# Splitting each weights' unit in one instruction per part instead of two, with a ring of two whole units

## The chip, the cores and the metric

One core of one Trainium2 chip runs the whole program. The metric is the device time of one execution in microseconds (us); of several executions the median counts. The engines are named as in the profile: PE is TensorE (PEld its weight loads), DVE is VectorE, ACT is ScalarE, POOL is GpSimd, and SP issues the DMA transfers.

## The reference

The input is 256 tokens of width 1024 in float32, batch 1. Two transformer-like stacks follow each other. The first has two layers: a mixer of a state-space branch and a neighbourhood attention, then an mLSTM mixer, each followed by an MLP. The second has one layer of three mixers, a cross attention and a gated MLP. What matters here is that nearly all of the work is a product of 256 tokens with a large float32 matrix:

```python
proj = h @ w_in                                          # mixers
u = jnp.square(jax.nn.relu(h @ mlp_w1[layer])) @ mlp_w2[layer]   # MLP of the first stack
a, b = jnp.split(h @ w_gu, 2, axis=-1)                   # gated MLP of the second stack
return (jax.nn.silu(a) * b) @ w_d
```

## The kernel before

**Units.** All weight matrices are cut on the host into 214 units of 128 partitions x 2048 float32 (1 MB each), in the order in which the program uses them. A unit is 256 columns of a matrix with 1024 rows, or 256 rows of one with 1024 columns. `unit(u, n)` brings one in: SP issues the DMA into a buffer `raw` (three of them, shared with the modulation weights `in_ada`), ACT writes a rounded copy `wh` (the high part, type fp32r), and DVE writes `wl = raw - wh` (the low part). A product of float32 accuracy is then made of three matmuls: high by high, high by low, low by high. The activations are split in the same way (`xh`, `xl`, or `mhh`, `mhl`, `ghh`, `ghl`, `yh`, `yl`).

**The ring.** `wh` and `wl` come from two pools that are used in rotation over the whole program. Before, a unit's part is two tiles of 1024 columns, and each pool has four tiles (`W_BUFS = 4`). A tile can be written again when the last matmul that reads it is done. 14 units (`fwh`, `fwl`: the fillers between the stages and some first units) have buffers of their own.

**The matmuls of a unit.** `proj_feat` and `proj_tok` make 48 matmuls of 256 columns: an outer loop over two halves of the output, an inner one over the eight blocks k of 128 rows, of which blocks 0 to 3 lie in the first tile and 4 to 7 in the second. So the first tile is read for the last time after 36 of the 48 matmuls, the second after all 48. `down` makes 24 matmuls of 512 columns, and there too the first tile is free after 18 of 24. `out_units` runs the last two units of a mixer's output matrix together: 12 matmuls of the one, 12 of the other, and then both again.

**The order.** The code is traced from top to bottom, and a scheduler then orders the instructions of each engine; each engine runs its own in order. Side work (state-space heads, attention heads, modulation vectors from `in_ada`, tables) is given out in steps between the units by `tick`. `held` keeps the first splits of a stage behind the last instructions of the norm before it, for all units but those marked `free` or with buffers of their own.

**Stages by time in the profile.** Start to 70 us, mixer0 70 to 272, norm and mlp0 272 to 490, mixer1 490 to 722, mlp1 722 to 925, mixer2 925 to 1250, cross attention to 1318, and the gated MLP to the end. In the MLPs an up unit (48 matmuls into `mm`) and a down unit (24 matmuls into `ax`) alternate; in the gated MLP there are two up units for one down unit.

Of the kernel before, what the change touches and what calls it, by code (L numbers as in the profile page):

```python
# [12 lines left out]
F32R = mybir.dt.float32r  # L13
I32 = mybir.dt.int32
AF = mybir.ActivationFunctionType
ALU = mybir.AluOpType
# [3 lines left out]
P = 128  # L20
# [2 lines left out]
NEG = -1.0e30  # L23
NOSYNC = mybir.DependencyInfo(mybir.DependencyClass.NoSync, mybir.DependencyReason.DATA)
RAW_BUFS = 3
W_BUFS = 4
NB_BUFS = 4

M0_ORDER = "aaaxxxaaaxbzaaazaaazz"
# [239 lines left out]
class Stack:  # L269
    def __init__(self, ctx, tc, aps):  # L270
# [3 lines left out]
        self.raw_p = pool("raw", RAW_BUFS)  # L274
        self.wh_p = pool("wh", W_BUFS)
        self.wl_p = pool("wl", W_BUFS)
        self.xT_p = pool("xT", 1)
# [153 lines left out]
    def unit(self, u, n, extra=False):  # L431
        if self.early > 0:
            extra, self.early = True, self.early - 1
        free = False
        if not extra and self.free > 0:
            free, self.free = True, self.free - 1
        raw = self.raw_p.tile([P, 2048], F32, tag="raw", name="raw")
        self.nc.sync.dma_start(out=raw, in_=self.a["wts"][u])
        hi, lo = [], []
        for i in range(2):  # L440
            src = raw[:, i * 1024:(i + 1) * 1024]
            if extra:
                h, l = self.pt("fwh", [P, 1024], F32R, 4), self.pt("fwl", [P, 1024], F32R, 4)
            else:
                h = self.wh_p.tile([P, 1024], F32R, tag="wh", name="wh")
                l = self.wl_p.tile([P, 1024], F32R, tag="wl", name="wl")
            with self.held(not extra and not free):
                self.act(h, src)
                self.tt(l, src, h, ALU.subtract)
            hi.append(h.rearrange("p (k n) -> p k n", n=n))  # L450
            lo.append(l.rearrange("p (k n) -> p k n", n=n))
        m = 1024 // n
        return [(hi[k // m][:, k % m], lo[k // m][:, k % m]) for k in range(2048 // n)]

    def small_unit(self, name):

# [1505 lines left out]
```

## Time and profile before

| what | value |
|---|---|
| median of 3 runs | 1512.66 us (1510.27 to 1514.73) |
| the profiled execution's own time | 1514.44 us |
| its span in the trace | 1512.3 us |
| mean granted TensorE clock | 0.992 |
| instructions in the span | 25366 |

The span is what the trace covers; the profiled execution's own time is 2.1 us longer. Durations below come from this one execution. Busy time of an engine is the time in which at least one of its instructions ran; the ends of matmuls are modelled, and they overlap each other.

### The profile page before, as it was taken

What the parts mean: (1) busy time and instruction counts of PE and PEld (TensorE: products, weight loads), DVE (VectorE), ACT (ScalarE), POOL (GpSimd) and SP (SyncE); (2) the same over time, 40 slices, a digit from 0 to 9 for tenths busy, and PEclk for the clock granted to TensorE, in tenths of its full rate; (3) what the DMA queues carried; (4) which work ended last, traced back from release to release, by engine and by line L of the source; (5) the groups of instructions that cost most, each with busy time, mean ns of one, the idle gap of its engine ahead of it and who ended that gap; (6) DMA issues with size and microseconds to landing.
All of it is one profiled execution on the core that took longest, in us unless ns stands there. A gap on an engine that the chain in (4) does not pass through costs nothing.

```text
span 1512.3 us, 25366 instructions
## 1 busy us (share of the span) xinstructions
PE 1432.1 (95%) x9932; PEld 1300.0 (86%) x9932; DVE 1162.8 (77%) x2223; ACT 854.2 (56%) x1502; POOL 12.1 (1%) x32
## 2 busy tenths in 40 slices
PE   2898999999999999999999999997999999999999
PEld 2886887898898899998889888976889989799998
DVE  7788978877777996666979858778999887565555
ACT  4686775554555665555746756555345457454443
POOL 0000000000000000000000000010000000000000
PEclk9999999999999999999999999999999999999999
DMA  8755887587876685445586664543443364245552
GB/s 348 257 176 164 281 304 261 199 293 273 335 299 233 255 299 194 170 140 183 210 302 221 238 210 176 192 156 119 148 146 140 140 239 179 84 165 174 191 187 93
DMA packets 63226, 316.53 MB, mean 209 GB/s; under 512 B 6521, under 2 KB 16385, under 8 KB 29314
## 3 DMA queue, kind: packets, MB, share of 16 engines
q1 hardware_dynamic: 63106, 314.90, 58.7%
q8 instruction: 78, 1.28, 0.3%
q14 instruction: 42, 0.34, 0.1%
HBM read 305.82 MB, written 9.06 MB: 208 GB/s over the span
## 4 chain that ended last, share of the span: by engine, by line
PE 68%; DVE 16%; DMA 7%; ACT 6%; issue 3%; POOL 0%; SPq 0%; ACTq 0%; DVEq 0%; POOLq 0%
PE mm L366 45%; PE ax L366 21%; DVE wl L360 3%; PE ax L370 2%; DMA raw<-in_wts 2%; DMA bp<-cs_d 2%; ACT wh L351 2%; DVE merged L360 1%; ACT xn L351 1%; DMA grow<-in_rows 1%; DVE s5w L373 1%; DVE s5w L360 1%; ACT nb L351 1%; DVE acc L638 1%; DMA bp<-nM_d 1%
## 5 line engine op out<-in xcount | busy, mean ns | idle before, releaser
L360 DVE TENSOR_TENSOR wl<-raw,wh 128x1024 fp32r<-128x1024 f32 x400 | 485.1, 1222 | 196.5 <-ACT wh L351 195.4
L351 ACT ACTIVATE wh<-raw 128x1024 fp32r<-128x1024 f32 x400 | 419.3, 1057 | 363.7 <-PE mm L366 225.7
L366 PE MATMUL mm<-xh,wl 128*128 128x256 f32 x1536 | 441.6, 288 | 12.2 <-DVE wl L360 12.1
L366 PE MATMUL mm<-xh,wh 128*128 128x256 f32 x1536 | 442.5, 288 | 6.7 <-ACT bp L351 2.8
L366 PE MATMUL mm<-xl,wh 128*128 128x256 f32 x1536 | 439.7, 286 | 0.0
L366 PEld LDWEIGHTS mm<-xh,wl 128*128 128x128 f32 x1536 | 298.0, 194 | 18.4 <-DVE wl L360 14.6
L366 PEld LDWEIGHTS mm<-xh,wh 128*128 128x128 f32 x1536 | 298.2, 194 | 12.4 <-ACT wh L351 4.1
L366 PEld LDWEIGHTS mm<-xl,wh 128*128 128x128 f32 x1536 | 298.1, 194 | 4.0 <-issue 2.3
L366 PE MATMUL mm<-wh,xh 128*128 128x256 f32 x496 | 143.3, 289 | 0.0
L366 PE MATMUL mm<-wl,xh 128*128 128x256 f32 x496 | 142.1, 286 | 1.2 <-DVE wl L360 1.1
L366 PE MATMUL mm<-wh,xl 128*128 128x256 f32 x496 | 141.2, 285 | 0.0
L366 PE MATMUL ax<-wh,mhh 128*128 128x512 f32 x256 | 102.4, 400 | 0.0
L366 PE MATMUL ax<-wl,mhh 128*128 128x512 f32 x256 | 101.3, 396 | 0.0
L366 PE MATMUL ax<-wh,mhl 128*128 128x512 f32 x256 | 101.3, 396 | 0.0
L366 PEld LDWEIGHTS mm<-wl,xh 128*128 128x128 f32 x496 | 95.4, 192 | 3.7 <-DVE wl L360 3.0
L366 PEld LDWEIGHTS mm<-wh,xh 128*128 128x128 f32 x496 | 95.3, 192 | 1.8 <-issue 1.0
L366 PEld LDWEIGHTS mm<-wh,xl 128*128 128x128 f32 x496 | 95.4, 192 | 0.6 <-issue 0.5
L366 PEld LDWEIGHTS ax<-wh,mhl 128*128 128x128 f32 x256 | 48.1, 188 | 12.0 <-DVE mhl L360 0.4
L366 PEld LDWEIGHTS ax<-wh,mhh 128*128 128x128 f32 x256 | 48.2, 188 | 10.7 <-ACT wh L351 0.5
L366 PEld LDWEIGHTS ax<-wl,mhh 128*128 128x128 f32 x256 | 48.1, 188 | 10.6 <-issue 0.5
L363 DVE SCALAR_TENSOR_TENSOR acc<-raw,cond,acc 128x1024 f32<-128x1024 f32 x28 | 35.8, 1277 | 8.1 <-DMA raw<-in_ada 7.9
L751 DVE CUSTOM_DVE_ANT_0 acc<-raw,crow 128x1024 f32<-128x1024 f32 x32 | 39.0, 1218 | 2.9 <-DMA raw<-in_ada 2.6
(489 smaller groups left out, 2511.7 us busy)
## 6 DMA issues: line engine op xcount, KB each, us to landing
raw<-in_wts SPq DMA_DIRECT2D x214, 1024.0 KB, 4.9
raw<-in_ada SPq DMA_DIRECT2D x48, 1024.0 KB, 5.5
nb<-in_nab SPq DMA_DIRECT2D x16, 256.0 KB, 5.8
grow<-in_rows SPq DMA_DIRECT2D x16, 256.0 KB, 6.2
bp<-cs_d SPq DMA_DIRECT2D x16, 256.0 KB, 5.2
s5tab<-s5t SPq DMA_DIRECT2D x16, 256.0 KB, 2.4
s5tl<-s5tab SPq DMA_DIRECT2D x16, 256.0 KB, 2.9
meml<-mem_d SPq DMA_DIRECT2D x2, 1024.0 KB
```

The costliest lines, as they stand in the source:

```text
L351: return self.nc.scalar.activation(out=out, in_=in_, func=func, **kw)
L360: return self.nc.vector.tensor_tensor(out=out, in0=in0, in1=in1, op=op)
L363: return self.nc.vector.scalar_tensor_tensor(out=out, in0=in0, scalar=s, in1=in1, op0=op0, op1=op1)
L366: return self.nc.tensor.matmul(out, lhsT, rhs, start=start, stop=stop)
L370: return self.nc.tensor.transpose(out, in_, self.ident[0:k, 0:k])
L373: return self.nc.vector.tensor_tensor_scan(out=out, data0=d0, data1=d1, initial=init, op0=op0, op1=op1)
L638: nc.vector.tensor_tensor_reduce(out=acc, in0=raw[:, k * D:(k + 1) * D], in1=self.crow, scale=1.0, scalar=0.0, op0=ALU.mult, op1=ALU.add, ...
L751: nc.vector.tensor_tensor_reduce(out=acc, in0=w, in1=self.crow, scale=1.0, scalar=0.0, op0=ALU.mult, op1=ALU.add, accum_out=s8[:, j:j + 1])
```

## The change

Each part of a unit becomes one tile of 2048 columns, made by one instruction: one ACT instruction for `wh`, one DVE instruction for `wl`. Each pool holds two such tiles, which take the same room as the four of before. The units with buffers of their own change in the same way (two tiles of 2048 for four of 1024). Nothing is computed otherwise, and the DMA of a unit stays one of 1 MB.

```diff
-W_BUFS = 4
+W_BUFS = 2
...
         raw = self.raw_p.tile([P, 2048], F32, tag="raw", name="raw")
         self.nc.sync.dma_start(out=raw, in_=self.a["wts"][u])
-        hi, lo = [], []
-        for i in range(2):
-            src = raw[:, i * 1024:(i + 1) * 1024]
-            if extra:
-                h, l = self.pt("fwh", [P, 1024], F32R, 4), self.pt("fwl", [P, 1024], F32R, 4)
-            else:
-                h = self.wh_p.tile([P, 1024], F32R, tag="wh", name="wh")
-                l = self.wl_p.tile([P, 1024], F32R, tag="wl", name="wl")
-            with self.held(not extra and not free):
-                self.act(h, src)
-                self.tt(l, src, h, ALU.subtract)
-            hi.append(h.rearrange("p (k n) -> p k n", n=n))
-            lo.append(l.rearrange("p (k n) -> p k n", n=n))
-        m = 1024 // n
-        return [(hi[k // m][:, k % m], lo[k // m][:, k % m]) for k in range(2048 // n)]
+        if extra:
+            h, l = self.pt("fwh", [P, 2048], F32R, 2), self.pt("fwl", [P, 2048], F32R, 2)
+        else:
+            h = self.wh_p.tile([P, 2048], F32R, tag="wh", name="wh")
+            l = self.wl_p.tile([P, 2048], F32R, tag="wl", name="wl")
+        with self.held(not extra and not free):
+            self.act(h, raw)
+            self.tt(l, raw, h, ALU.subtract)
+        hi, lo = (a.rearrange("p (k n) -> p k n", n=n) for a in (h, l))
+        return [(hi[:, k], lo[:, k]) for k in range(2048 // n)]
```

The scheduler orders the changed program anew. Three places show what stands where. The first is DVE at the start of mlp0, where the norm ends with the two `xl` of its last token block and the first two ring units of the stage follow. Before:

```order
L357 TENSOR_SCALAR nf_3094<-mm_3089,mod0_107 128x128
L360 TENSOR_TENSOR xl_2978<-nf_3081,xh_2977 128x4x128
L700 CAST xh_2977<-nf_3094 128x4x128
L360 TENSOR_TENSOR xl_2978<-nf_3094,xh_2977 128x4x128
L360 TENSOR_TENSOR wl_3256<-raw_3253,wh_3255 128x1024
L360 TENSOR_TENSOR wl_3260<-raw_3253,wh_3259 128x1024
L360 TENSOR_TENSOR wl_3323<-raw_3320,wh_3322 128x1024
```

And in the changed program:

```order
L357 TENSOR_SCALAR nf_2974<-mm_2969,mod0_107 128x128
L360 TENSOR_TENSOR xl_2858<-nf_2961,xh_2857 128x4x128
L695 CAST xh_2857<-nf_2974 128x4x128
L360 TENSOR_TENSOR xl_2858<-nf_2974,xh_2857 128x4x128
L360 TENSOR_TENSOR wl_3128<-raw_3125,wh_3127 128x2048
L360 TENSOR_TENSOR wl_3191<-raw_3188,wh_3190 128x2048
```

Nothing moved: the split follows the last `xl` in both, in one instruction where there were two. The second place is ACT in the steady part of mlp0, where `wh` alternates between down and up units and `mr`, `mhh`, `msq` work on the result of an up unit (`mr` reads its PSUM tile `mm`). Before:

```order
L351 ACTIVATE wh_4308<-raw_4306 128x1024
L351 ACTIVATE wh_4312<-raw_4306 128x1024
L351 ACTIVATE wh_4347<-raw_4345 128x1024
L351 ACTIVATE mr_4292<-mm_4233 128x512
L351 ACTIVATE wh_4351<-raw_4345 128x1024
L351 ACTIVATE mhh_4295<-mr_4292 128x512
L351 ACTIVATE msq_4294<-mr_4292 128x512
L351 ACTIVATE wh_4417<-raw_4415 128x1024
```

And in the changed program (the down unit is 4106, the up unit 4141):

```order
L351 ACTIVATE wh_4108<-raw_4106 128x2048
L351 ACTIVATE wh_4143<-raw_4141 128x2048
L351 ACTIVATE mr_4092<-mm_4037 128x512
L351 ACTIVATE mhh_4095<-mr_4092 128x512
L351 ACTIVATE msq_4094<-mr_4092 128x512
L351 ACTIVATE wh_4209<-raw_4207 128x2048
```

The up unit's `wh`, which waits for the same matmuls as `mr` does, stands ahead of `mr` whole; before, its second half stood behind it. The third place is PE at the end of mixer1's output matrix, where the last two units run together (before 7652 with 7656, then 7662 with 7666; `mm_7363` to `mm_7366` are the four accumulators). Before, where the second unit comes in after the first one's 12 matmuls on the first token block:

```order
L366 MATMUL mm_7364<-wh_7656,yh_7359 128x512
L366 MATMUL mm_7364<-wl_7657,yh_7359 128x512
L366 MATMUL mm_7364<-wh_7656,yl_7360 128x512
L366 MATMUL mm_7363<-wh_7662,yh_7569 128x512
L366 MATMUL mm_7363<-wl_7663,yh_7569 128x512
L366 MATMUL mm_7363<-wh_7662,yl_7570 128x512
```

And in the changed program (first unit 7268, second unit 7274), where the second unit's low part is first read after 28 matmuls of the pair, 24 of them the first unit's:

```order
L366 MATMUL mm_7006<-wh_7268,yh_6999 128x512
L366 MATMUL mm_7006<-wl_7269,yh_6999 128x512
L366 MATMUL mm_7006<-wh_7268,yl_7000 128x512
L366 MATMUL mm_7005<-wh_7274,yh_7193 128x512
L366 MATMUL mm_7006<-wh_7274,yh_7193 128x512
L366 MATMUL mm_7003<-wl_7275,yh_7193 128x512
L366 MATMUL mm_7003<-wh_7274,yl_7194 128x512
```

The first unit's second token block moved ahead of the second unit's low part.

## Rows read from the trace of the kernel before

**Rows 1.** The page, part 1: busy time of each engine
```profile
PE 1432.1 (95%) x9932; PEld 1300.0 (86%) x9932; DVE 1162.8 (77%) x2223; ACT 854.2 (56%) x1502; POOL 12.1 (1%) x32
```
**Rows 2.** The page, part 4: the chain that ended last, by engine
```profile
PE 68%; DVE 16%; DMA 7%; ACT 6%; issue 3%; POOL 0%; SPq 0%; ACTq 0%; DVEq 0%; POOLq 0%
```
**Rows 3.** The page, part 5: the two groups that split the ring units
```profile
L360 DVE TENSOR_TENSOR wl<-raw,wh 128x1024 fp32r<-128x1024 f32 x400 | 485.1, 1222 | 196.5 <-ACT wh L351 195.4
L351 ACT ACTIVATE wh<-raw 128x1024 fp32r<-128x1024 f32 x400 | 419.3, 1057 | 363.7 <-PE mm L366 225.7
```
**Rows 4.** Groups by form: the same two operations over 512 columns
```profile
L360 DVE TENSOR_TENSOR mhl<-msq,mhh 128x512 fp32r<-128x512 f32 x32 | 22.0, 687 | 4.3 <-ACT msq L351 4.3
L351 ACT ACTIVATE mhh<-mr 128x512 fp32r<-128x512 f32 x32 | 20.1, 629 | 0.5
```
**Rows 5.** The chain in time, 1355 to 1400 us: start, us, what
```profile
1371.95 5.60 PE ax L366 x24
1377.55 11.50 PE mm L366 x96
```
**Rows 6.** Timeline of ACT there: start, us, instruction [idle before <- releaser]
```profile
1370.48 1.06 ACT L351 ACTIVATE wh<-raw 128x1024 fp32r<-128x1024 f32 x1 [0.75 <-PE mm L366]
1371.93 1.06 ACT L351 ACTIVATE wh<-raw 128x1024 fp32r<-128x1024 f32 x1 [0.39 <-PE mm L366]
1372.89 0.36 ACT L351 ACTIVATE gth<-mm 128x256 f32<-128x256 f32 x1
```
**Rows 7.** Timeline of DVE there
```profile
1371.57 1.23 DVE L360 TENSOR_TENSOR wl<-raw,wh 128x1024 fp32r<-128x1024 f32 x1 [1.38 <-ACT wh L351]
1373.02 1.23 DVE L360 TENSOR_TENSOR wl<-raw,wh 128x1024 fp32r<-128x1024 f32 x1 [0.23 <-ACT wh L351]
```
**Rows 8.** Timeline at the start of mlp0: ACT, DVE and PE
```profile
293.45 3.90 ACT L351 ACTIVATE wh<-raw 128x1024 fp32r<-128x1024 f32 x4
...
295.58 4.62 DVE L360 TENSOR_TENSOR wl<-raw,wh 128x1024 fp32r<-128x1024 f32 x4
...
296.45 0.39 PE L366 MATMUL mm<-xh,wh 128*128 128x256 f32 x1 [1.15 <-ACT wh L351]
...
296.85 0.38 PE L366 MATMUL mm<-xh,wl 128*128 128x256 f32 x1
```
**Rows 9.** Timeline of DVE at the start of mixer1
```profile
497.39 2.35 DVE L360 TENSOR_TENSOR wl<-raw,wh 128x1024 fp32r<-128x1024 f32 x2
```
**Rows 10.** Waits over the whole span: us in total, times, longest
```profile
ACT wh L351 <- DMA raw<-in_wts: 48.5, 18, 5.4
...
PE mm L366 <- DVE wl L360: 13.3, 11, 6.2
```
**Rows 11.** Waits of PE from 925 to 1250 us
```profile
PE mm L366 <- DVE wl L360: 10.4, 5, 6.2
```
**Rows 12.** Around 382 us in mlp0: ACT, DVE, and the chain
```profile
381.56 2.01 ACT L351 ACTIVATE wh<-raw 128x1024 fp32r<-128x1024 f32 x2 [0.93 <-DMA raw<-in_wts]
...
382.65 4.82 DVE L360 TENSOR_TENSOR wl<-raw,wh 128x1024 fp32r<-128x1024 f32 x4 [1.29 <-ACT wh L351]
...
384.41 5.74 PE mm L366 x48
```
**Rows 13.** Windows: span, PE, PEld, DVE, ACT, POOL busy (instructions), clock, DMA share, GB/s
```profile
70.00:272.00 202.00, 189.98 (x1309) 161.84 (x1309) 173.89 (x379) 139.49 (x301) 0.00 (x0) 0.99 0.70 238
300.00:490.00 190.00, 189.97 (x1203) 170.21 (x1203) 140.59 (x191) 100.58 (x137) 0.00 (x0) 1.00 0.79 290
925.00:1250.00 325.00, 305.62 (x2391) 282.31 (x2389) 277.58 (x529) 165.97 (x268) 9.73 (x12) 0.97 0.45 158
```
**Rows 14.** The chain in time, 50 to 72 us
```profile
49.54 1.06 ACT wh L351
...
51.91 0.42 ACT kb L351
```
**Rows 15.** The chain in time, 704 to 722 us
```profile
704.85 11.21 PE mm L366 x48
```

## The prediction

> **What bounds the kernel now.** I read the busy times first: PE is busy for 95% of the span, DVE for 77%, ACT for 56% [rows 1]. The chain that ended last is 68% PE, but 16% DVE, 7% DMA and 6% ACT [rows 2]. So the kernel as a whole is bound by matmuls, and somewhat under a third of it hangs on other things, which are found stage by stage. The table of windows tells the stages apart [rows 13]: in mlp0 PE runs without a hole, while in mixer0 and mixer2 DVE is busy for 174 of 202 and 278 of 325 us, 86% and 85%. A merged split can pay only where DVE or ACT is on the path, and can hurt only where a split comes last. The waits show how little of that there is now: PE waits for `wl` 11 times, 13.3 us in all, 10.4 of it in mixer2 [rows 10, 11], and ACT waits for a late `raw` 18 times, 48.5 us in all [rows 10].
>
> **The price of one instruction.** DVE takes 687 ns for 512 columns [rows 4] and 1222 for 1024 [rows 3]: 1.045 ns a column and 152 ns fixed, so 2048 columns take about 2.29 us. ACT takes 629 and 1057 ns [rows 3, 4]: 0.836 ns a column and 201 fixed, so 1.91 us. Two halves alone cost 2.44 and 2.11 us, so at most 0.15 and 0.20 us is saved per unit. But back to back two `wl` end in 2.35 us [rows 9] and two `wh` in 2.01 [rows 12]: most of the fixed part already lies under the neighbour. What is saved there is 0.06 us on DVE and 0.10 on ACT.
>
> The Trainium skill ("VectorE: DVE Perf Modes", section on the TRN2 errata) says that an SBUF operand costs a fixed latency per instruction, which one large tile pays once and many small ones each; by it every one of the 200 ring units would be cheaper. The rows agree in the direction, and put most of the saving at the overlapped price.
>
> **What becomes later.** A split is a chain: ring tile free, `wh`, `wl`, matmul. For a unit's first low part it was 1.06 + 0.03 + 1.22 = 2.31 us (a single `wh`, then its `wl` 0.03 behind [rows 6, 7]), and will be 1.91 + 0.03 + 2.29 = 4.23, that is 1.92 later. Where DVE was busy anyway and `wh` long done, only 2.29 - 1.22 = 1.07 of that shows. Besides, the ring tile is no longer free after three quarters of the unit two before, but at its end.
>
> In the steady stretches this hides. In the gated MLP the unit in rows 6 and 7 had its first `wh` at 1370.48 and its first low part at 1372.80, for matmuls that begin at 1377.55 when the down unit ends [rows 5 to 7]: 4.75 us early. Now its tile is free at 1371.95, when the up units end [rows 5], its low part is there at 1371.95 + 4.23 = 1376.18, still 1.37 us early. A down unit of 5.60 us is the shortest cover, up units take 5.75 each [rows 5]. In the new order ACT's `wh` stands ahead of `mr` and its followers, so nothing comes in between. I cost the steady part at 0; with the cover gone it would be a loss on every such pair. The `raw` buffer is also given back later, at 1376.18 instead of 1374.25, the end of the second `wl` [rows 7]; DMA, busy for 79% of mlp0 [rows 13], has two other buffers to fill meanwhile, and I cost this at 0 as well.
>
> **Term A, starts of stages.** At mlp0 DVE's last `xl` gives way to `wl` at 295.58, the first low part is ready at 296.80, and PE reads it at 296.85 [rows 8]. In the new order the split stands at the same place, so it is ready at 297.87: 1.07 us later, and PE has nothing else. `wh` is no obstacle: it runs from 293.45 [rows 8] and would end at 295.36. At mixer1 it is the same from 497.39 [rows 9], and the start of mlp1 reads alike. Three times 1.07 = 3.2 us.
>
> **Term B, late transfers.** Where `raw` lands late, ring and engines are idle and the whole 4.23 counts. Around 382 us `wh` waits for the DMA until 381.56, `wl` follows at 382.65, and the chain's 48 matmuls begin at 384.41 [rows 12]. The new low part comes at 381.56 + 4.23 = 385.79, after PE has run dry. The 18 waits [rows 10] lie in four stretches (late in mixer0 and in mlp0, early in mixer1 and in mlp1). Within a stretch the next transfer is late anyway, so the delay shows once, by its last late unit: 4 x 1.92 = 7.7 us. A and B give 10.9; the bounds are 7 x 1.07 = 7.5, if the starts' price holds in all seven places, and 7 x 1.92 = 13.4.
>
> **Term C, the start of the program.** ACT's `wh` of 1.06 us at 49.54 lies on the chain, ahead of `kb` [rows 14]. A merged one costs 0.85 more there: +0.9, bounds 0 and 2.7 (three such).
>
> **Term D, ends of output matrices.** The last unit's low part would come 1.4 us late if it were read after the first 12 matmuls, 12 x 0.234 = 2.8 us, by 48 in 11.21 us [rows 15]. But in the new order it is first read after 28, 6.5 us: 0.
>
> **Term E, the mixers that DVE bounds.** 63 ring units lie in mixer0 and mixer2. If DVE is on the path throughout, they give 63 x 0.06 = 3.8 us, or 63 x 0.15 = 9.6 if no pair stood back to back; if never, nothing. DVE is busy for 86% there, but in part beside PE: I take half of the overlapped price, -1.9, with bounds -9.6 and 0. The five waits for `wl` in mixer2 [rows 11] I take as unchanged, since there DVE's sequence, not one split's latency, sets the pace; if each grew by 1.92, they would add 9.6.
>
> **Sum.** 10.9 + 0.9 - 1.9 = +9.9 us, on the profiled execution's own 1514.44: 1524.3. That execution was 1.8 above the median of 1512.66, so **1522.5 us**. The forecast's own range is +5 to +16, or 1517.5 to 1528.5.
>
> **The rivals.** *Slower still, the ring locks.* 1.37 us of slack is less than three ACT operations on 512 columns (`mr`, `mhh`, `msq`, 3 x 0.63 = 1.89 by `mhh` [rows 4]). If they run ahead of a `wh`, the low part is 0.5 us late for 32 up units [rows 4]: 16 us more, near 1538, up to 1545 with mixer2's five waits. For it: the margin shrinks from 4.75 to 1.37. Against: the new order of ACT has `wh` first. *Faster, the saved fixed cost wins.* If DVE sets the pace of the mixers and the single price holds, E gives 9.6; if the starts are absorbed besides, by a transfer that PE waits for later anyway, only 2 to 4 us of A to C remain: about -5 to -8, 1505 to 1508. It decides from the point at which E passes the 11.8 of A to C or these shrink below it. For it: 16% of the chain is DVE [rows 2]. Against: pairs already overlap [rows 9]. *No change.* PE moves other work over the later split (attention and state-space matmuls, or other `raw` units already split), each of the seven places hides most of its 1 to 2 us, and E takes the rest: 1509 to 1516. For it: what is asked for is 1 to 2 us at a time, and in the mixers PE has small matmuls to run. Against: at a stage's start every matmul hangs on the same norm, and rows 8 show PE waiting right there.
>
> The Trainium skill ("Perfetto Trace Analysis", section Optimizing Scalar/DVE Operations) names both sides: grouping helps if the engine is saturated, and where Scalar or Vector are not, but cause bubbles on other engines, breaking instructions up lets work complete sooner. By ACT's 56% and DVE's 77% [rows 1] the second half of that rule holds for most of this kernel, which is the side of my forecast; by the 85% of the mixers the first would give the rival that is faster.
>
> **How the numbers follow.** A measurement of this kernel can tell about 0.3% from no change, 4.5 us: 1508.1 to 1517.2 counts as the same. The forecast has 0.44, since A and B rest on places seen in the trace and on an order that is known. The ring that locks has 0.16, the faster case 0.18, no change 0.22. Slower: 0.44 + 0.16 = 0.60. The range for 8 in 10 reaches from the upper end of the faster case to the lower end of the locked ring, 1508 to 1538: it leaves out half to most of the faster case and half of the locked one.
>
> **What would show it.** `wl` near 2.29 us and `wh` near 1.91 in the groups; PE's first low-part matmul of mlp0 about 1.1 us further behind its last `xl`; PE waiting for `wl` at the starts and behind late transfers, some 20 us in all instead of 13.3; no regular gap between up and down units in the gated MLP. A regular gap there would show the locked ring. If DVE's share in the mixers falls and mixer2 ends sooner by several us, E was too small. I am wrong if the late transfers shift (they depend on when `raw` buffers come free), or if the new order puts mixer2's DVE work so that its five waits grow or vanish.

## The result, and the profile after

The changed kernel takes 1557.37 us (median of 4 runs, 1555.3 to 1561.27) against 1511.56 us before (4 runs, 1510.27 to 1514.73): a ratio of 1.029, with a 95% interval of 1.0269 to 1.0311. It is 45.8 us slower; the range had ended at 1538. The profiled execution took 1555.99 us; its trace spans 1553.9 us, 41.6 more than the trace before, and these 41.6 us are what the rest of this section divides.

The page of the changed kernel, parts 1, 4 and 5, in the lines that answer to [rows 1 to 3]:

```profile
PE 1448.9 (93%) x9932; PEld 1314.8 (85%) x9932; DVE 1144.4 (74%) x2009; ACT 821.2 (53%) x1288; POOL 15.1 (1%) x32
...
PE 69%; DVE 15%; DMA 7%; ACT 6%; issue 3%; POOL 0%; SPq 0%; ACTq 0%; DVEq 0%; POOLq 0%
...
L360 DVE TENSOR_TENSOR wl<-raw,wh 128x2048 fp32r<-128x2048 f32 x200 | 457.8, 2289 | 227.0 <-ACT wh L351 226.6
L351 ACT ACTIVATE wh<-raw 128x2048 fp32r<-128x2048 f32 x200 | 382.6, 1914 | 309.5 <-PE mm L366 202.0
```

The prices were right: 2289 and 1914 ns. The merged instructions also did save work: DVE is busy 1162.8 - 1144.4 = 18.4 us less, ACT 854.2 - 821.2 = 33.0 us less. None of it reached the end. The shares of the chain are those of before within a point, so by them no other engine became the bound. PE itself is busy 1448.9 - 1432.1 = 16.8 us longer with the same 9932 matmuls, and so idle 24.8 us longer. Two views show where. The waits of PE in the changed kernel, which answer to [rows 10] (engine and what it waited for; us in total, times, longest):

```profile
PE mm L366 <- DVE wl L360: 25.1, 17, 3.7
...
PE mm L366 <- ACT wh L351: 14.6, 11, 3.9
```

Waits for `wl` are up from 13.3 to 25.1 us. Those for `wh` were a small thing before, as its own list of PE's waits says:

```profile
PE mm L366 <- ACT wh L351: 2.8, 2, 1.7
```

Together that is 39.7 instead of 16.1 us, or 23.6 more, nearly all that PE is idle longer. The other 18 of the 41.6 us are almost the 16.8 that its matmuls took longer. With that goes the clock: the mean granted TensorE clock is 0.975, against 0.992 in the trace before. The windows of the changed kernel for the start of the program and around the starts of mlp0, mixer1 and mlp1 (span; busy us and instructions of PE, PEld, DVE, ACT, POOL; granted clock, DMA share, GB/s):

```profile
0.00:70.00 70.00, 38.24 (x259) 36.57 (x260) 51.14 (x112) 38.41 (x63) 0.68 (x10) 0.88 0.83 310
276.50:307.50 31.00, 28.21 (x180) 25.26 (x179) 27.44 (x77) 17.99 (x43) 0.00 (x0) 0.94 0.48 177
501.40:545.00 43.60, 37.12 (x279) 35.62 (x278) 37.11 (x60) 21.88 (x29) 0.17 (x3) 0.92 0.69 243
741.00:769.50 28.50, 24.45 (x178) 24.25 (x179) 24.27 (x92) 18.17 (x46) 0.00 (x0) 0.88 0.46 155
```

The same stretches had 1.00 before. These three seams hold about a third of the clock lost against the trace before, the first 70 us another third, the mixers and the cross attention the rest. How much of the 16.8 us is clock isn't told apart here, since the ends of matmuls are modelled; and the kernel before had mean clocks from 0.983 to 0.994 in its executions beside the experiments, the changed kernel's four had 0.974 to 0.977.

**The steady stretches** did what was forecast. In the gated MLP, ACT, DVE and the chain of the changed kernel at the unit that answers to [rows 5 to 7] (start, us, instruction; the chain: start, us, what):

```profile
1413.48 1.92 ACT L351 ACTIVATE wh<-raw 128x2048 fp32r<-128x2048 f32 x1 [0.28 <-PE mm L366]
```

DVE:

```profile
1415.43 2.29 DVE L360 TENSOR_TENSOR wl<-raw,wh 128x2048 fp32r<-128x2048 f32 x1 [1.78 <-ACT wh L351]
```

The chain:

```profile
1402.02 11.50 PE mm L366 x96
1413.51 5.60 PE ax L366 x24
1419.11 1.90 PE mm L366 x16
```

The low part is ready at 1415.43 + 2.29 = 1417.72 and is read from 1419.11: 1.39 us early, where 1.37 was forecast. PE runs without a hole, in the same 11.50 and 5.60 us.

**Where the 41.6 us are.** The same 214 units run in the same order of units in both programs. So the end of the last matmul of each unit can be compared between two traces, and the growth of the difference from the last unit of one stage to that of the next is what the stage lost. The first column does this for the changed kernel; the others are the experiments of the next section, each against the same trace of before. Each column is the one execution that was traced; programs that agree in a stage can differ there by 3 to 4 us (the rest of mlp0: 3.9 in the changed kernel, over 7 in e9 and e13).

| us lost to the kernel before | changed | e2 | e3 | e4 | e8 | e10 | e5 |
|---|---|---|---|---|---|---|---|
| start | 2.2 | 2.2 | 3.2 | 5.9 | 6.0 | 6.1 | 8.4 |
| mixer0 | 2.3 | -5.2 | -3.1 | 0.8 | 2.0 | 12.5 | 38.1 |
| start of mlp0 | 3.0 | 0.5 | 2.0 | 0.0 | 1.1 | 0.0 | 2.6 |
| rest of mlp0 | 3.9 | 0.0 | 0.0 | 0.9 | 2.7 | 0.2 | 8.1 |
| fillers, start of mixer1 | 3.7 | 3.5 | 2.2 | -1.1 | 1.4 | 1.3 | 1.2 |
| rest of mixer1 | 3.9 | 1.4 | 4.5 | 0.6 | 0.7 | 7.8 | 21.1 |
| fillers, start of mlp1 | 5.5 | 3.0 | 1.5 | 1.4 | 1.4 | 1.5 | 4.9 |
| rest of mlp1 | -0.2 | 0.3 | 3.1 | 0.5 | 1.0 | 1.9 | 8.2 |
| fillers, mixer2 | 9.0 | 4.6 | 5.2 | 0.9 | 3.5 | 33.3 | 60.1 |
| cross attention | 7.3 | 5.2 | 6.3 | 0.0 | -0.1 | 2.8 | 7.5 |
| gated MLP | 1.0 | 0.1 | 1.1 | 0.7 | 1.6 | 1.4 | 5.4 |
| sum | 41.6 | 15.5 | 25.9 | 10.7 | 21.2 | 68.9 | 165.7 |

Most of the first column lies at seams and in stages with much side work; mlp1 once it runs and the gated MLP lose next to nothing. Three places show how a hole comes about.

*Start of mlp0.* DVE and PE of the changed kernel, which answer to [rows 8]:

```profile
299.91 0.69 DVE L360 TENSOR_TENSOR xl<-nf,xh 128x512 fp32r<-128x512 f32 x1
300.52 4.49 DVE L360 TENSOR_TENSOR wl<-raw,wh 128x2048 fp32r<-128x2048 f32 x2
```

PE:

```profile
302.86 0.39 PE L366 MATMUL mm<-xh,wl 128*128 128x256 f32 x1 [0.21 <-DVE wl L360]
303.09 0.29 PE L366 MATMUL mm<-xh,wh 128*128 128x256 f32 x1
303.20 0.39 PE L366 MATMUL mm<-xl,wh 128*128 128x256 f32 x1
303.39 0.42 PE L366 MATMUL mm<-xh,wl 128*128 128x256 f32 x1
```

From the first `wl` to PE's first matmul with it: 302.86 - 300.52 = 2.34 us, before 296.85 - 295.58 = 1.27 [rows 8]. The difference is 1.07, term A to the hundredth. But the stage lost 3.0: the norm itself came 0.5 later, and right behind the wait the same 256-column matmuls take 0.42 instead of 0.28 us. That is the clock (granted 0.53 from 303.0 to 306.5 us), and the start of mlp1 shows it whole. There PE waits 1.82 us for the low part, and then:

```profile
760.28 0.39 PE L366 MATMUL mm<-xh,wl 128*128 128x256 f32 x1 [1.82 <-DVE wl L360]
...
761.06 0.41 PE L366 MATMUL mm<-xh,wh 128*128 128x256 f32 x1
761.27 0.41 PE L366 MATMUL mm<-xl,wh 128*128 128x256 f32 x1
...
764.16 0.28 PE L366 MATMUL mm<-xh,wh 128*128 128x256 f32 x1
764.28 0.28 PE L366 MATMUL mm<-xl,wh 128*128 128x256 f32 x1
```

Matmuls start 0.21 us apart instead of 0.12 (granted clock 0.72 from 758 to 764 us, the wait included). From 760.63 to 764.04 there are 16 steps, which cost 3.41 instead of 1.92 us: the wait of 1.82 cost 1.5 us more.

*Cross attention.* Here the split is ahead of work that is ready. ACT and DVE of the changed kernel:

```profile
1313.08 1.91 ACT L351 ACTIVATE wh<-raw 128x2048 fp32r<-128x2048 f32 x1 [1.92 <-PE mm L366]
1314.90 0.82 ACT L351 ACTIVATE xq<-mm,xgain 128x256 f32<-128x256 f32 x2
1315.61 0.59 ACT L351 ACTIVATE xyh<-ax 128x512 fp32r<-128x512 f32 x1
```

DVE:

```profile
1315.03 2.29 DVE L360 TENSOR_TENSOR wl<-raw,wh 128x2048 fp32r<-128x2048 f32 x1 [4.99 <-ACT wh L351]
1317.24 0.68 DVE L360 TENSOR_TENSOR xyl<-ax,xyh 128x512 fp32r<-128x512 f32 x1
```

`wh` stands at the head of ACT and waits 1.92 us for PE, since its tile is free only when the unit two before ends. DVE stands idle for 4.99 us at `wl`, and the head's `xq`, `xyh`, `xyl` and the small norm operations stand behind 1.91 and 2.29 us of a split whose low part PE first reads 23 us after it is ready (at 1340.50). The chain runs over that split. From the start of `wh` to PE's next small product it takes 1320.39 - 1313.08 = 7.31 us, and before it took 1282.23 - 1277.03 = 5.20. Before:

```profile
1277.03 1.06 ACT wh L351
...
1282.23 0.44 PE mm L370 x2
```

And in the changed kernel:

```profile
1313.08 1.92 ACT wh L351
...
1320.39 0.69 PE mm L370 x2
```

The place in the order does most of this, not the length: in e2, whose two halves stand at the same place, the stage loses 5.2 of these 7.3 us.

### The profile page after: what moved, and what is told of

It is laid out like the page before. It is cut to its first block, busy times and chain, and to the rows that moved or that the text cites. A ratio compares the mean times of both kernels' runs of the same rounds, so it can differ in the third digit from the quotient of the medians.

```text
span 1553.9 us, 24756 instructions
## 1 busy us (share of the span) xinstructions
PE 1448.9 (93%) x9932; PEld 1314.8 (85%) x9932; DVE 1144.4 (74%) x2009; ACT 821.2 (53%) x1288; POOL 15.1 (1%) x32
## 4 chain that ended last, share of the span: by engine, by line
PE 69%; DVE 15%; DMA 7%; ACT 6%; issue 3%; POOL 0%; SPq 0%; ACTq 0%; DVEq 0%; POOLq 0%
PE mm L366 48%; PE ax L366 19%; DVE wl L360 4%; ACT wh L351 3%; DMA raw<-in_wts 2%; DMA raw<-in_ada 2%; PE ax L370 1%; DVE merged L360 1%; DMA bp<-cs_d 1%; DVE s5w L373 1%; DVE s5w L360 1%; DVE acc L633 1%; DVE acc L746 1%; ACT xn L351 1%; PE mm L370 0%
## 5 line engine op out<-in xcount | busy, mean ns | idle before, releaser
L360 DVE TENSOR_TENSOR wl<-raw,wh 128x2048 fp32r<-128x2048 f32 x200 | 457.8, 2289 | 227.0 <-ACT wh L351 226.6
L351 ACT ACTIVATE wh<-raw 128x2048 fp32r<-128x2048 f32 x200 | 382.6, 1914 | 309.5 <-PE mm L366 202.0
L366 PE MATMUL mm<-xh,wh 128*128 128x256 f32 x1536 | 446.8, 291 | 15.6 <-ACT wh L351 12.5
L366 PEld LDWEIGHTS mm<-xh,wl 128*128 128x128 f32 x1536 | 302.2, 197 | 26.0 <-DVE wl L360 23.2
L366 PEld LDWEIGHTS mm<-xh,wh 128*128 128x128 f32 x1536 | 302.2, 197 | 22.8 <-ACT wh L351 14.6
L366 PEld LDWEIGHTS mm<-xl,wh 128*128 128x128 f32 x1536 | 302.3, 197 | 5.2 <-issue 3.5
```

What stands on the lines that cost most here:

```text
L351: return self.nc.scalar.activation(out=out, in_=in_, func=func, **kw)
L360: return self.nc.vector.tensor_tensor(out=out, in0=in0, in1=in1, op=op)
L366: return self.nc.tensor.matmul(out, lhsT, rhs, start=start, stop=stop)
```

## The experiments

How the order was held. In some runs each engine issues its instructions in the order of another program. A table of that order stands in the kernel's file, and each instruction gets an edge to the one ahead of it on its engine, for the order of issue alone:

```diff
+def in_order(tc):
...
+        for a, b in zip(at[:-1], at[1:]):
+            tc.add_manual_dep(seq[b], seq[a].name,
+                              mb.DependencyInfo(mb.DependencyClass.NoSync, mb.DependencyReason.DATA), reason="order")
```

All results, as ratios to the kernel before on the same chip:

| run | splits | ring | order | us | ratio (95%) |
|---|---|---|---|---|---|
| changed | merged | 2 units | new | 1557.4 | 1.029 (1.0269 to 1.0311) |
| e1 | merged, at the second half's place | 2 units | old | 1670.8 | 1.1024 (1.0978 to 1.107) |
| e5 | merged, at the first half's place | 2 units | old | 1673.1 | 1.104 (1.0993 to 1.1087) |
| e10 | halves | 2 units | old | 1583.0 | 1.0449 (1.0428 to 1.0471) |
| e2 | halves | 4 halves | new | 1531.9 | 1.0122 (1.0073 to 1.0172) |
| e3 | halves | 2 units | new | 1541.0 | 1.0164 (1.0124 to 1.0205) |
| e11 | high part merged | 2 units | new | 1549.3 | 1.0239 (1.0206 to 1.0273) |
| e12 | low part merged | 2 units | new | 1561.4 | 1.0318 (1.0274 to 1.0362) |
| e4 | halves | 2 units | its own | 1525.1 | 1.007 (1.0046 to 1.0094) |
| e8 | merged in the MLPs alone | 2 units | its own | 1534.5 | 1.0135 (1.0095 to 1.0175) |
| e6 | high part merged | 2 units | its own | 1550.7 | 1.0241 (1.0204 to 1.0278) |
| e7 | low part merged | 2 units | its own | 1580.2 | 1.0435 (1.04 to 1.047) |
| e9 | merged | 2 units | new, old at two seams | 1561.9 | 1.032 (1.0283 to 1.0357) |
| e13 | merged | 2 units | new, splits moved at two places | 1559.1 | 1.0301 (1.0277 to 1.0326) |
| e14 | halves | 4 halves | old, new in mixer0 | 1512.6 | 0.9996 (0.9979 to 1.0012) |

**Order against latency.** The first theory after the result was that the scheduler's new order of norms and side work makes the loss ('order'); its rival, that the longer and later split makes it, whatever the order ('latency').

e1, merged splits in the old order: 

> The changed kernel (one ACT and one DVE instruction of 2048 columns per unit, ring of two units), but every engine issues its instructions in the order of the kernel before; each merged split stands at the place of its unit's second half (for one unit in mixer2, at that of the first). Theory 'order': most of the 46 us comes from the new order that the scheduler chose for norms and side work, so this is near my terms A to E, 1515 to 1527 us. Theory 'latency': the longer, later split itself costs the 46 us, at starts of stages and in mixer2, whatever the order: 1545 us or more.

Measured 1670.8. 'Order' is out; 'latency' had the side, but this is 113 us above the changed kernel with the same splits and ring. e5 asks whether the chosen place did it:

> As the run of the merged split in the old order, but each merged split stands at the place of its unit's first half (for one unit in mixer0, at that of the second), so it is never asked for later than the first half was. Theory 'order' (the scheduler's new order makes the loss): 1515 to 1530 us. Theory 'place' (halves stood apart, with other work between them, and no single place in an order made for halves suits a split of 2048 columns): 1540 us or more, the loss in the mixers now as ACT and DVE work that waits behind the longer split. Theory 'latency': as 'place', but with PE waiting for wl as often as in the changed kernel.

Measured 1673.1, the same, as 'place' had it. So the theory 'order' in its plain form fell: the old order doesn't save the changed kernel, it is far worse for it than the new one, and the new order is what keeps the loss as small as it is. The table of stages says where: 38, 21 and 60 us in the three mixers, where most side work stands among the splits. The waits of e5 over the whole span, against 195.4 and 225.7 us before [rows 3]:

```profile
DVE wl L360 <- ACT wh L351: 334.2, 147, 8.4
ACT wh L351 <- PE mm L366: 300.9, 99, 10.4
```

Both engines stand longer at the head of a split, with everything that follows in their order behind it. The sign that 'latency' had named for this run is there too: PE waits for `wl` 18 times, 23.2 us in all, against 17 times and 25.1 us in the changed kernel. But that is a small part of the 160 us. e2, e3 and e10 split this up.

e2, the old halves and ring in the new order: 

> The kernel before (two halves per part, ring of four halves), but every engine issues its instructions in the order of the changed kernel; the two halves stand back to back at the place of the merged split. Theory 'order': 1535 to 1555 us, the loss comes without any merged instruction. Theory 'latency': 1510 to 1520 us, since split and ring are those of before.

Measured 1531.9, between the two. The new order alone costs 18 us (1.0122, by its interval 11 to 26), with splits that are as short as before. By the table it loses at the starts of mixer1 and mlp1 and in the cross attention, and it wins 5 us in mixer0. e3 adds the ring's grain, a tile that is free only when its whole unit has been read:

```diff
+            h = self.wh_p.tile([P, 2048], F32R, tag="wh", name="wh")
+            l = self.wl_p.tile([P, 2048], F32R, tag="wl", name="wl")
+        for i in range(2):
+            cs = slice(i * 1024, (i + 1) * 1024)
+            with self.held(not extra and not free):
+                self.act(h[:, cs], raw[:, cs])
+                self.tt(l[:, cs], raw[:, cs], h[:, cs], ALU.subtract)
```

> As the run before (halves, order of the changed kernel), but the two halves lie in one tile of a ring of two units, which is free only at the unit's end. Against that run it tells the ring's grain alone, and against the changed kernel (1557) the merged instruction alone, both in one order. Theory 'order': within 5 us of the run before, and the merged instruction on top gives the rest to 1557. Theory 'latency by the ring': 10 us or more slower than the run before; 'latency by the instruction': as the run before, 20 us or more faster than the changed kernel.

Measured 1541.0, 1.0164: some 6 us above e2, with intervals that overlap. From e3 to the changed kernel only the merging is left, and it costs 1.029 - 1.0164 = 0.0126, or 19 us. In the new order the three parts are thus about 18 (order), 6 (ring, not clear of the scatter) and 19 us (instructions). By the table, merging costs 5.4 us of this in mixer0 (2.3 against -3.1), 3.8 in mixer2 and 6.5 at the three starts; the other rows cancel out.

e10, the ring's grain alone in the old order: 

> The kernel before in its own order, with its halves, each at its place (but for one unit of mixer0, where they stand together); only the ring's grain is changed: two halves share one tile of a ring of two units, which is free at the unit's end. Theory 'the ring's grain': most of the 160 us that the merged split lost in the old order comes from here, since a split that must wait for the unit's end stands in ACT's order ahead of work that PE needs: 1630 us or more. Theory 'the instruction's length': 1515 to 1540 us.

Measured 1583.0, between the two: in the old order the grain costs 68 us and the merged instructions 90 more. Both parts of the change are dear in an order made for halves.

**Which instruction.** e6 and e7, each in an order of its own:

```diff
+            self.act(h, raw)
+            for cs in (slice(0, 1024), slice(1024, 2048)):
+                self.tt(l[:, cs], raw[:, cs], h[:, cs], ALU.subtract)
```

e7:

```diff
+            for cs in (slice(0, 1024), slice(1024, 2048)):
+                self.act(h[:, cs], raw[:, cs])
+            self.tt(l, raw, h, ALU.subtract)
```

> Ring of two whole units, own order; only the high part is made in one instruction, the low part in two halves. First low part 1.91 + 0.03 + 1.22 = 3.2 us after a free tile, against 2.3 with halves and 4.2 merged. Theory 'latency': between the halves (1525) and the changed kernel (1557) by that share, 1535 to 1545 us. Theory 'order': any time from 1515 to 1560, with the losses at places of its own.

> Ring of two whole units, own order; only the low part is made in one instruction, the high part in two halves ahead of it. First low part 2.0 + 0.03 + 2.29 = 4.3 us after a free tile, as in the changed kernel, while the first high part comes 0.85 us sooner. Theory 'latency': 1550 to 1560 us, as the changed kernel. Theory 'order': any time from 1515 to 1560, and not above the run with the high part merged for the reason of latency.

Measured 1550.7, above what latency asked for, and 1580.2. The low part is the dearer one, but 1580 is more than the changed kernel with both merged, which latency alone doesn't explain. The same in the new order:

> Order of the changed kernel, ring of two units, high part merged, low part in two halves back to back. Between e3 (both in halves, 1541) and the changed kernel (both merged, 1557) with order and ring the same. Theory 'latency of the chain': the first low part comes 0.85 us later than in e3 and 1.07 sooner than merged, so 1546 to 1550. Theory 'DVE is what is late': 1541 to 1544.

> Order of the changed kernel, ring of two units, high part in two halves, low part merged. Theory 'latency of the chain': the merged low part must wait for both halves of the high part, 0.1 us later than in the changed kernel, while the first high part is 0.85 sooner: 1553 to 1558. Theory 'the merged run with the low part alone (1580) was slow by its own order': this one is at least 20 us below it; if not, the low part merged alone is slow in itself.

Measured 1549.3 (runs from 1540.65 to 1554.99) and 1561.4. Over e3 the merged high part costs 0.0075, or 11 us, the merged low part 0.0154, or 23 us. The first time lies in the range that latency asked for, the second 3 us above it. The two don't add up to the 19 us of both together: the low part merged alone is as slow as both, within the scatter. e12 is 19 us below e7, where at least 20 were asked for if the fault was e7's own order; so most of the 23 us by which e7 lies above the changed kernel is that order. An order that the scheduler makes for itself can thus cost (e7 against e12) or save (e4, below, against e3) an amount that no price of the changed operation tells.

**Ring alone, and where merging hurts.** e4 is the code of e3 without a table:

> Halves in a ring of two whole units, in the order that the scheduler chooses for it. Theory 'order': each new order is a draw of its own, so the time may lie anywhere from 1510 to 1560 us, and what it loses lies at other places than in the changed kernel. Theory 'latency by the ring': 1540 us or more; 'latency by the instruction': 1510 to 1520 us.

Measured 1525.1 (1.007), outside the ranges of both 'latency' theories, while 'order' allowed nearly any time. Where the scheduler may fit the order to it, the grain costs 11 us, in the trace more than half of it at the start of the program. That is 16 us less than e3, the same splits and ring in the changed kernel's order. e8 merges only where the unit is one of an MLP's:

```diff
+        m = 2048 if 38 <= u < 70 or 102 <= u < 134 or u >= 183 else 1024
+        for cs in (slice(i, i + m) for i in range(0, 2048, m)):
```

> Ring of two whole units, own order; both parts merged in the units of the three MLPs alone (ring units), halves in the mixers, the cross attention and the fillers. By the trace of the changed kernel the MLPs' steady stretches lose nothing once they run, mlp0 some 4 us and each MLP's start about 3. Theory 'latency at the places where a split comes last': 1528 to 1535 us, 3 to 10 above the halves in a ring of two units (1525). Theory 'order': 1515 to 1560.

Measured 1534.5, in the range of the theory of the places where a split comes last. That isn't proof of it: 'order' allowed this time too, and of the 10.5 us by which its trace exceeds e4's only 4.3 lie in the rows of the three MLPs, where it merges. This run shows term A clean at the start of mlp0, since the mixer ahead is in halves. DVE and PE of e8 at the start of mlp0:

```profile
303.57 4.49 DVE L360 TENSOR_TENSOR wl<-raw,wh 128x2048 fp32r<-128x2048 f32 x2
```

PE:

```profile
305.91 0.39 PE L366 MATMUL mm<-xh,wl 128*128 128x256 f32 x1 [0.20 <-DVE wl L360]
306.13 0.28 PE L366 MATMUL mm<-xh,wh 128*128 128x256 f32 x1
306.25 0.28 PE L366 MATMUL mm<-xl,wh 128*128 128x256 f32 x1
```

Again 2.34 us from split to matmul, 1.07 more than before; the matmuls behind it take 0.28 us, and the stage's start loses 1.1 us in the table. So the same 1.07 cost 1.1 us here and, with a norm that was 0.5 late and a lower clock, 3.0 in the changed kernel. At the start of mlp1 e8 loses 1.4, no more than e4 does with halves.

**The seam between mixer1 and mlp1.** In the changed kernel the pair of last output units runs in another order (the third place of the section on the change). There it lost nothing to a late low part, but its two token blocks end together, and PE waits 2.55 us for the norm's `x`:

```profile
743.23 0.39 PE L366 MATMUL mm<-fwh,memh 128*128 128x256 f32 x1 [2.55 <-DVE x L363]
```

e9 puts the pair, the norm and the fillers back into the old order among themselves, there and at the seam before mixer1:

> The changed kernel in its own order, but at two seams (end of mlp0 to mixer1, end of mixer1 to mlp1) the last pair of output units, the norm and the fillers stand among themselves in the order of the kernel before; the splits keep their places. Theory 'order': the 5 us that each of the two seams loses in the trace and the 3 us behind the second (lower clock) come back, 8 to 13 us: 1544 to 1549. Theory 'latency': the seams wait for the later splits whatever the norm's order, 1554 to 1560.

Measured 1561.9: nothing came back. From the unit before the pair to the second unit of mlp1 the changed kernel loses 5.5 us and e9 5.1; the loss only moved. PE of e9, and the windows (span; busy us and instructions of PE, PEld, DVE, ACT, POOL; granted clock, DMA share, GB/s):

```profile
737.38 0.50 PE L366 MATMUL mm<-wl,yh 128*128 128x512 f32 x1 [2.23 <-DVE wl L360]
```

The windows:

```profile
738.50:741.50 3.00, 3.00 (x8) 2.35 (x8) 1.73 (x2) 0.69 (x2) 0.00 (x0) 0.50 1.01 404
741.50:744.50 3.00, 3.00 (x14) 2.38 (x14) 1.77 (x8) 0.69 (x2) 0.00 (x0) 0.99 0.99 396
```

Now PE waits 2.23 us for the last unit's low part, and then runs for 3 us at a clock of 0.50, with 8 matmuls where the next 3 us hold 14. ACT and DVE of e9 say why the low part is late:

```profile
730.89 1.90 ACT L351 ACTIVATE fwh<-raw 128x2048 fp32r<-128x2048 f32 x1
732.70 1.90 ACT L351 ACTIVATE wh<-raw 128x2048 fp32r<-128x2048 f32 x1
```

DVE:

```profile
732.83 2.29 DVE L360 TENSOR_TENSOR fwl<-raw,fwh 128x2048 fp32r<-128x2048 f32 x1 [1.32 <-ACT fwh L351]
735.04 2.28 DVE L360 TENSOR_TENSOR wl<-raw,wh 128x2048 fp32r<-128x2048 f32 x1
```

A filler's split, wanted only when both token blocks are done, stands ahead of the one that PE waits for. e13 moves it behind:

```diff
-L351 ACTIVATE fwh<-raw 128x2048
-L351 ACTIVATE wh<-raw 128x2048
-L351 ACTIVATE fwh<-raw 128x2048
+L351 ACTIVATE wh<-raw 128x2048
+L351 ACTIVATE fwh<-raw 128x2048 x2
```

> The changed kernel in its own order, changed at two places only. End of mixer1: last output pair, norm and fillers in the order of the kernel before (as in e9), and the filler's merged split (fwh, fwl), which stood ahead of the last output unit's on ACT and DVE, goes right behind it. Start of mixer1: the first wh ahead of kc, the first wl ahead of the modulation vector's acc. Theory 'a long split blocks what stands behind it': the low part of the last output unit is ready some 1.3 us sooner than in e9, and the stretch from the unit before the pair to the second unit of mlp1 loses 3 to 4 us to the kernel before, instead of 5.5 in the changed kernel and 5.1 in e9; mixer1's start loses 3.5 to 4 instead of 5.1. Theory 'only the 4.2 us from a free tile to the low part count': both stretches as in e9. In all 1550 to 1560 us either way.

PE of e13 at the same matmul:

```profile
736.46 0.50 PE L366 MATMUL mm<-wl,yh 128*128 128x512 f32 x1 [1.34 <-DVE wl L360]
```

The window behind it:

```profile
736.40:739.40 3.00, 2.94 (x13) 2.40 (x14) 3.00 (x3) 2.04 (x4) 0.00 (x0) 1.00 0.62 221
```

The wait is 1.34 us, the clock stays up, and the stretch loses 3.6 us instead of 5.1. From the last filler to mixer1's first unit it loses 4.2 instead of 5.1, a little more than was expected. So at this place a merged split did block what stood behind it, and another order mended it; the whole time, 1559.1, doesn't show it against the scatter.

**Can an order alone win?** 

> Halves and ring of the kernel before, and its order, but for the start and mixer0, whose instructions stand among themselves in the order of the changed kernel; e2's trace reached the end of mixer0 3.1 us sooner than the kernel before in that order. Theory 'the order alone can win a stage': 1508 to 1513 us, a ratio of 0.996 to 0.999. If that 3.1 came from one execution or from what surrounds mixer0: 1513 to 1520.

Measured 1512.6, a ratio of 0.9996 (0.9979 to 1.0012). Its one trace is 5.0 us shorter than that of before, and reaches the end of mixer0 3.3 us sooner, as e2's did (3.1). But twelve runs say the same time, with an interval from 3.2 us faster to 1.8 slower. So a gain of 3 us is neither shown nor quite excluded; no version here is shown to beat the kernel before. A ring of three whole units was not tried.

## Why the prediction was wrong, point by point

- **Prices and the steady part: right.** 2289 and 1914 ns; 1.39 us of slack where 1.37 was forecast, and no stall in the gated MLP or in mlp1 once it runs. The ring did not lock there.
- **Term A (three starts at 1.07): right in its mechanism at mlp0, too small.** The 1.07 is there in the changed kernel and in e8. But the three starts lost 3.0, 3.7 and 5.5 us with the fillers, 12.2 instead of 3.2. With halves in the same order (e3) they lose 2.0, 2.2 and 1.5, so merging itself costs 6.5 there and the order and the ring's grain the rest: a norm or a pair of units that ends later, other work ahead of the split, and a lower clock behind waits. "At mixer1 it is the same" did not hold: `wh`, which stood ahead of `kc` before, stands behind it, PE waits 3.90 us for it, and `wl` stands behind 1.22 us of a modulation vector's work. ACT, DVE and PE of the changed kernel there:

```profile
508.83 0.62 ACT L351 ACTIVATE kc<-ax 128x512 f32<-128x512 f32 x1
509.30 3.74 ACT L351 ACTIVATE wh<-raw 128x2048 fp32r<-128x2048 f32 x2
...
512.12 2.29 DVE L360 TENSOR_TENSOR wl<-raw,wh 128x2048 fp32r<-128x2048 f32 x1
...
511.30 0.48 PE L366 MATMUL mm<-xh,wh 128*128 128x256 f32 x1 [3.90 <-ACT wh L351]
```

- **Term B (late transfers, 7.7): not told apart.** The rest of mlp0 lost 3.9 and mixer0 2.3, mlp1 nothing, which is the forecast's size at most. The late transfers themselves shifted: ACT waits for `raw` 11 times, 34.0 us in all, instead of 18 and 48.5 [rows 10]. The same stretch of mlp0 lost over 7 in e9 and e13, in the same order of splits, so it varies by several us between executions.
- **Term C (start, 0.9): 2.2**, inside its bounds of 0 and 2.7, but by luck: e2, with the old halves and ring, loses the same 2.2 there, so this is not shown to be the price of a merged `wh`.
- **Term D (ends of output matrices, 0): wrong.** It asked only when the low part is first read. That PE reads it after 28 matmuls instead of 12 has a price of its own: the first token block's accumulators end with the second's, and the norm that follows is late (e2, with halves in this order, loses 3.0 there too). e9 and e13 price the alternative that the prediction had worked out, 1.4 us late after 12 matmuls: 1.34 us in e13, and 2.23 with a filler's split ahead.
- **Term E (mixers, -1.9): wrong in sign.** DVE did save 18.4 us of busy time, but mixer0 lost 2.3 and mixer2 with its fillers 9.0, and over e3, in one order, merging alone cost 5.4 and 3.8. So DVE's 85% in them did not make its throughput the path. What the chain shows at one place, and what is argued for the others, is that PE and DVE hand small results to and fro, and a longer split between two of them is a delay, whatever it saves in sum. The place is in mixer2, where `wl` stands behind 9 us of state-space and norm work and PE behind `wl`; in e3's chain the `wl` there takes 1.14 us instead of 2.20:

```profile
1020.71 0.58 DVE qks L901
...
1021.97 2.20 DVE wl L360
...
1024.22 0.79 PE mm L366 x2
```

- **The cross attention (no term at all): 7.3 us.** By e2 and e3 (5.2 and 6.3) most of it is the new order, and by e4 and e8 (0.0 and -0.1) other orders avoid it.

The step that failed is the one that took "an order that is known" for the reason to trust the sum: the prediction read the new order at three places, for the splits alone, and priced every other move at nothing. e2 puts the price of these moves at 18 us. The second step was to price lateness only where a split already came last. A merged split also makes late what stands behind it on ACT and DVE and on the chain (mixer2's `wl` above, the seam of e9 and e13), which was named under "nothing comes in between" for the MLPs and never asked for the mixers; in the new order merging costs 19 us, against the 10 of the whole forecast. The third was to leave the clock out. The mean granted clock is 0.975 for 0.992; at half rate in the low stretches that is (0.025 x 1553.9 - 0.008 x 1512.3) = 26.7 us of lost clock at most, if PE had been busy throughout; PE's busy time grew by 16.8, and at the start of mlp1 it is 1.5 us on top of a wait of 1.82.

Of the rivals, the one that is slower still had the right side and the wrong place: the slack of the MLPs held, and the mixers and seams, which it named only by "mixer2's five waits", gave way. (Its upper figure should have been 1548, not 1545: 1538 and the 9.6 of the five waits.) The rule of the Trainium skill that the prediction weighed ("Perfetto Trace Analysis", section Optimizing Scalar/DVE Operations), that breaking instructions up can let work complete sooner where Scalar and Vector are not saturated but cause bubbles on other engines, is what e3 against the changed kernel shows, at 19 us. By its other half, that grouping helps if the engine is saturated, the mixers should have gained if 85% of DVE counts as that; mixer0 and mixer2 lost, 5.4 and 3.8 us over e3.

What stays open: how much of the new order's 18 us belongs to which move, since only two seams were changed one at a time, and why the scheduler's own order with the low part alone merged (e7) is so much worse than the others.

## What to carry to other kernels

Engines that run their instructions in order paid here for a longer one twice: at its own reader, and at all that stands behind it and is ready; so a merge is to be priced at every place where the engine has small work on a chain, not only by its saved fixed cost and the slack of its reader. Where a scheduler orders the program, a changed size can be a new order everywhere, and a trace of before says little of it: here two orders of one program differed by about 1% (1.2% from the kernel before to e2, 0.9% between e3 and e4, 1.2% between e7 and e12), which belongs into the range. To tell order from price, hold the order and change the instruction, and then the other way round.

## What the runs showed of the hardware

The clock's part was not expected in this size. After PE had waited 1.82 us (start of mlp1, changed kernel) or 2.23 us (e9) PE ran slowly for about 3 us: in e9 at a granted clock of 0.50, the lower of the two levels (1.2 of 2.4 GHz), in the changed kernel with matmuls 0.21 us apart instead of 0.12. After 1.34 us in e13, at the same place of the program as e9's, it stayed up at 1.00. At the start of mlp0 the waits were nearly the same in two programs, and the clock was not: 0.83, 1.29 and 0.21 us in the changed kernel, then 0.53 from 303.0 to 306.5 us; 0.35, 1.30 and 0.20 us in e8, and 1.00 from 302 to 308. So holes of nearly one size can differ by about 1.5 us in what they cost; what decided it is not shown here.

The saving by merging was a little larger than the price of neighbours back to back: 18.4 us over 214 units is 0.086 us each on DVE (0.06 forecast), and 33.0 us is 0.154 each on ACT (0.10).
